# Low parts of the mixers' weight chunks: every fourth one subtracted on GpSimd instead of VectorE

## The chip, the cores and the metric

The kernel runs on one core of a Trainium2 chip. The metric is the device time of one execution in microseconds (us). TensorE is PE in the profile, VectorE is DVE, ScalarE is ACT, GpSimd is POOL, SyncE is SP. Numbers that enter a large product are kept in two parts here: a high part, rounded to the format fp32r, and the low part that the rounding leaves over.

## The reference

256 tokens of width 1024 go through two blocks. The first block has two layers, each a mixer, a layer norm, a feed-forward part (dense in layer 0, eight experts with two chosen per token in layer 1) and another layer norm:

```python
def mixer_block(x, w_in, ...):
    p_swa, p_rwkv, p_fox, p_dsa, p_gate = split_cols(x @ w_in, IN_GROUPS)
    o_swa = swa_branch(*split_cols(p_swa, SWA_SPLITS), sinks)
    o_rwkv = rwkv7_branch(p_rwkv, mu, w0, w_up, a0, a_up, g_up, k_k, k_a, r_k, gn_g, gn_b)
    o_fox = fox_branch(*split_cols(p_fox, FOX_SPLITS), f_bias)
    o_dsa = dsa_branch(*split_cols(p_dsa, DSA_SPLITS))
    gates = jax.nn.sigmoid(p_gate.reshape(B, S, N_BRANCHES, D_MODEL) + gate_bias)
    w_rows = split_cols(w_branch, MIX_WIDTHS, axis=0)
    for i, (o, w) in enumerate(zip((o_swa, o_rwkv, o_fox, o_dsa), w_rows)):
        merged = merged + gates[:, :, i] * (o @ w)
    return merged @ w_out

def first_block(x, ...):
    for layer in range(DEPTH):
        y = mixer_block(x, w_in[layer], ...)
        x = layer_norm(DN_ALPHA * x + y, ln_g[layer, 0], ln_b[layer, 0])
        ...
```

`swa` is attention in a window with sinks, `rwkv7` a recurrence of matrix states with a group norm and a gate at its end, `fox` attention with forget gates, `dsa` attention to the 64 best of the keys that an index score picks. The second block (a mixer of MoBA and gMLP, gated linear attention, cross-attention, SwiGLU) is not touched by the change.

## The kernel before, in words

**Products.** The tokens are two tiles of 128 (`t` = 0, 1). Every activation that enters a weight product is kept as a high part and a low part (`xh`, `xl`), and so is every weight (`H`, `L`). `lin` (L550 on) and `lin_fm` (L576 on) issue three matmuls per step: `xh`·`H`, `xl`·`H`, `xh`·`L`. The third one needs the low part of the weight.

**Weight chunks.** `load` (L512 to L531) brings one chunk, at most 128 x 1024 numbers: SyncE starts its DMA into a half of a `raw` tile (four such halves in the mixers), ScalarE copies it in fp32r into `wh` (through `act`, L445), and VectorE subtracts, `raw` − `wh`, into `wl` (through `sub` and `tt`, L458). There are six pairs of `wh` and `wl`; a pair is free again after the last matmul that reads it (`done`).

**The mixers.** A mixer sets `woven` (`weave`, L425). Its 68 chunks are then loaded ahead, at most four (`LOOK = 4`), as pairs come free (`fill`, `take`). TensorE's instructions and SyncE's weight DMAs keep the order of the program (`keep_in_program_order`); the other engines' order is set by a scheduler, which is why an edit of one helper can move instructions elsewhere. Between the projections the generators of the recurrence (`rwkv_tile`, L1052), `dsa` (L993), `fox` (L954) and `swa` (L941) are pumped on, each step's small products and row operations lying among the large products. Mixer 0 takes the first 305 us of the span, mixer 1 about the stretch from 510 to 830 us.

**Helpers that the steps below name.** `tt` (L458) is a two-input operation of VectorE, `stt` (L455) one with a scalar too, `ts` (L450, L452) one with one input; all run on VectorE unless an engine is passed. `groupnorm` (L1297) ends the recurrence of a tile: sums (L1299, L1307), an inverse root by small operations, then products on 128x256; the product with the gate follows, and TensorE transposes it (L382). `dsa` picks by eight rounds of `max` and `match_replace` (L1019, L1020). `ln_apply` (L1347) normalises tile 0, transposes it and splits it, and then tile 1. GpSimd makes masks at the start (L642, L730), clears buffers for the recurrence (L1180, L1213) and starts some DMAs (L1062, L1063, L1344).

**Holding.** `held` (L533) keeps the subtractions of the next mixer out of a layer norm: after tile 0 is split, `ln_apply` sets `hold = (last, 2)`, so the next two subtractions are free and the following ones may issue only after `last`. `self.last` names the last subtraction, and `rwkv` (L1041) lets three small operations of its constants issue after it.

Of the kernel before, what the change touches and what calls it, by code (L numbers as in the profile page):

```python
# [11 lines left out]
F32 = mybir.dt.float32  # L12
# [77 lines left out]
def specs():  # L90
    sp = {}
    for l in range(2):
        sp[f"win{l}"] = std_chunks(D, win_blocks())
        sp[f"wbr{l}"] = [_kch(_r(k, k + n), b) for k, n in ((0, 4), (4, 2), (6, 2), (8, 2)) for b in _blocks(D)]
        sp[f"wout{l}"] = kfirst_chunks(D, _blocks(D))
        sp[f"xq{l}"] = std_chunks(D, _blocks(D))
        sp[f"xkv{l}"] = std_chunks(D, _blocks(2 * D))
        sp[f"xo{l}"] = kfirst_chunks(D, _blocks(D))
        gu = []
        for b in _short_second(FF):  # L100
            for o in (0, FF):
                gu.append(_kch(_r(0, 8), [c + o for c in b]))
        sp[f"gu{l}"] = gu
        sp[f"dn{l}"] = down_chunks(FF)
    sp["w1"] = std_chunks(D, _short_second(FF))
    sp["w3"] = std_chunks(D, _short_second(FF))
    sp["w2"] = down_chunks(FF)
    sp["evin"] = std_chunks(D, _blocks(2560))
    sp["evo"] = kfirst_chunks(D, _blocks(D))
    sp["odin"] = std_chunks(D, _blocks(3072))  # L110
    sp["odo"] = kfirst_chunks(D, _blocks(D))
    sp["rw"] = [[(_r(0, 8), _r(0, 8))]]
    sp["odg1"] = [[(_r(0, 8), _r(0, 16))]]
    for e in range(8):
        sp[f"e1_{e}"] = std_chunks(D, _short_first(1408))
        sp[f"e3_{e}"] = std_chunks(D, _short_first(1408))
        sp[f"e2_{e}"] = down_chunks(1408)
    return sp
# [82 lines left out]
class Arena:  # L201
# [4 lines left out]
    def __init__(self, tiles, small=0, fit=0):  # L206
        self.t = tiles
        self.small, self.fit = small, fit
        self.at = [np.zeros(t.shape[-1] // self.U, np.int64) for t in tiles]
        self.clock = 0  # L210
        self.used, self.peak = 0, 0
# [51 lines left out]
class Net:  # L263
    def __init__(self, ctx, tc, a, out):
        self.tc, self.nc, self.a, self.out = tc, tc.nc, a, out
        self.sp = specs()
        self.off = {}
        self.cst = ctx.enter_context(tc.tile_pool(name="cst", bufs=1))
        pool = ctx.enter_context(tc.tile_pool(name="ar", bufs=1))
        block = lambda n, dt, w=CH: pool.tile([128, w], dt, name=n, tag=n)  # L270
        self.arena = Arena([block(f"af{i}", F32) for i in range(AF_BLOCKS)], small=SMALL)
        self.arenar = Arena([block("ars", F32R, AR_SMALL)] + [block(f"ar{i}", F32R) for i in range(AR_BLOCKS)], small=8, fit=64)
        self.raws = deque()
        for i in range(RAW):
            r = block(f"raw{i}", F32)
            self.raws.extend(r[:, j:j + RW] for j in range(0, CH, RW))
        self.pairs = deque()
        for i in range(0, PAIRS, 2):
            h, l = block(f"wh{i}", F32R), block(f"wl{i}", F32R)
            self.pairs.extend((h[:, j:j + RW], l[:, j:j + RW]) for j in range(0, CH, RW))  # L280
        self.extra = []
        self.pp = ctx.enter_context(tc.tile_pool(name="pp", bufs=4, space=PSUM))
        self.first = None
        self.hold, self.remap = (None, 0), {}
        self.ahead = AHEAD
        self.woven, self.vt, self.chains, self.loaded, self.todo = False, 0.0, [], deque(), deque()
        self.keys, self.scopes, self.cur = {}, [], None

# [208 lines left out]
    def block(self, name, b, lazy=False):  # L497

        if name not in self.off:
            o, l = 0, []  # L500
            for blk in self.sp[name]:
                l.append([])
                for k, c in blk:
                    l[-1].append(o)
                    o += 128 * len(k) * len(c)
            self.off[name] = l
        if self.woven and not lazy:
            return [partial(self.take, name, c) for c in self.off[name][b]]
        ws = [partial(self.load, name, *c) for c in zip(self.sp[name][b], self.off[name][b])]
        return ws if lazy else [w() for w in ws]  # L510

    def load(self, name, chunk, off):  # L512
        ks, cols = chunk
        ap = self.a[name]
        m = len(ks) * len(cols)
        src = bass.AP(tensor=ap.tensor, offset=ap.offset + off, ap=[[m, 128], [1, m]])
        w = Weight(self.pairs.popleft(), ks, len(cols))
        w.id = name, off
        raw = self.raws.popleft()
        dma = self.nc.sync.dma_start(out=raw[:, :m], in_=src)  # L520
        if self.woven:
            self.tc.keep_in_program_order(dma)
        h, lo = w.pair[0][:, :m], w.pair[1][:, :m]
        with self.tc.high_priority(self.ahead):
            with self.tc.issue_after(self.first.ins) if self.first else nullcontext():
                self.act(h, raw[:, :m])
            with self.held():
                self.last = self.sub(lo, raw[:, :m], h.bitcast(F32))
        self.raws.append(raw)
        return w  # L530

# [1568 lines left out]
```

## Time and profile before

| | |
|---|---|
| median of 3 runs | 2142.77 us |
| the runs | 2140.14 to 2144.49 us |
| the profiled execution | 2144.34 us |
| its span, first to last instruction | 2142.6 us |
| instructions | 31352 |
| mean granted clock of TensorE, of full speed | 0.982 |

The times that the sections below work with are those of the profiled execution, counted from the start of its span. A timeline row gives the start, the time busy, the engine, the line, the operation, what it writes and reads (buffer numbers left out), and in brackets the engine's idle time just before and what ended it. Rows of equal instructions that follow each other are one row with their count. Chunks are counted from 0 in each mixer, in the order of their loading.

### The profile page before, as it was taken

The page shows a single profiled execution, that of the slowest core. Times are in us where ns is not written, and L with a number is a line of the kernel's source. Part 1 is how long each engine was busy: PE and PEld are TensorE (multiplying, and loading weights), DVE is VectorE, ACT ScalarE, POOL GpSimd, SP SyncE. Part 2 cuts the span into 40 slices and gives each one's busy share as a digit, 9 for nine tenths or more (in the row PEclk, how much of TensorE's full clock was granted, in tenths as well). Part 3 has the DMA queues.
Part 4 walks back from the last instruction along what each step waited for, and adds up shares of the span by engine and source line. Part 5 has one row for each costly group of instructions (what it writes and reads, how often), then busy time and mean ns, then how long its engine had stood idle before and what let it go on. Part 6 is the DMA issues. An engine that isn't in the chain of part 4 may idle for free. (4 is left out here: it accounts for less than half of the span.)

```text
span 2142.6 us, 31352 instructions
## 1 busy us (share of the span) xinstructions
PE 2074.1 (97%) x11520; PEld 1699.4 (79%) x11520; DVE 1514.8 (71%) x2952; ACT 1138.3 (53%) x1684; POOL 43.1 (2%) x115
## 2 busy tenths in 40 slices
PE   8989999998998999999999998999999999999999
PEld 7867777886986777888888887877888777778887
DVE  6776677556667579988888898977645657676454
ACT  5433444443444345677777785575544454555442
POOL 1000000000000000000000000000000000000000
PEclk9999999999999999999999999999999999999999
DMA  6532474552544345699999997536555353654561
GB/s 227 173 94 86 156 251 148 187 188 78 171 136 124 106 141 195 222 345 333 344 339 327 333 316 237 170 127 210 178 188 187 105 171 117 205 181 164 177 197 59
DMA packets 118450, 411.91 MB, mean 192 GB/s; under 512 B 13648, under 2 KB 13808, under 8 KB 118288
## 3 DMA queue, kind: packets, MB, share of 16 engines
q1 hardware_dynamic: 113184, 392.91, 54.9%
q0 software_dynamic: 5104, 16.92, 2.5%
q8 instruction: 92, 1.51, 0.3%
q14 instruction: 70, 0.57, 0.1%
HBM read 408.72 MB, written 1.05 MB: 191 GB/s over the span
## 5 line engine op out<-in xcount | busy, mean ns | idle before, releaser
L379 PE MATMUL mm<-wh,ar 128*128 128x512 f32 (+3 forms) x3200 | 982.0, 388 | 11.1 <-PEq L1670 5.1
L379 PEld LDWEIGHTS mm<-wh,ar 128*128 128x128 f32 x3200 | 588.0, 190 | 126.9 <-issue 14.5
L458 DVE TENSOR_TENSOR wl<-raw,wh 128x1024 fp32r<-128x1024 f32 (+3 forms) x464 | 547.5, 1192 | 182.9 <-ACT wh L445 173.3
L445 ACT ACTIVATE wh<-raw 128x1024 fp32r<-128x1024 f32 (+3 forms) x464 | 476.1, 1035 | 279.0 <-PE mm L379 157.3
L379 PE MATMUL mm<-wl,ar 128*128 128x512 f32 (+3 forms) x1600 | 614.7, 384 | 0.0
L458 DVE TENSOR_TENSOR wl<-af,wh 128x1024 fp32r<-128x1024 f32 (+2 forms) x300 | 347.2, 1173 | 151.7 <-ACT wh L445 141.5
L445 ACT ACTIVATE wh<-af 128x1024 fp32r<-128x1024 f32 (+2 forms) x300 | 303.7, 1020 | 153.6 <-PE mm L379 56.3
L379 PE MATMUL ps<-wh,ar 128*128 128x512 f32 x1104 | 349.8, 394 | 2.3 <-ACT ar L445 2.3
L379 PEld LDWEIGHTS mm<-wl,ar 128*128 128x128 f32 x1600 | 304.1, 190 | 55.5 <-issue 0.8
L379 PEld LDWEIGHTS ps<-wh,ar 128*128 128x128 f32 x1104 | 206.3, 188 | 44.8 <-ACT ar L445 3.9
L379 PE MATMUL ps<-wl,ar 128*128 128x512 f32 x552 | 215.4, 390 | 0.0
L379 PE MATMUL mm<-ar,wh 128*128 128x256 f32 x704 | 139.2, 298 | 4.5 <-ACT ar L445 2.7
L382 PE MATMUL pr<-ident,af 128*128 128x128 f32 x584 | 97.8, 290 | 39.6 <-DVE af L458 24.7
L445 ACT ACTIVATE ar<-pr 128x512 fp32r<-128x512 f32 (+1 forms) x118 | 65.9, 567 | 115.3 <-PE pr L382 100.1
L382 PEld LDWEIGHTS pr<-ident,af 128*128 128x128 f32 x584 | 69.7, 146 | 71.4 <-issue 40.1
L379 PEld LDWEIGHTS mm<-ar,wh 128*128 128x128 f32 x704 | 115.0, 200 | 8.8 <-ACT ar L445 3.4
L379 PEld LDWEIGHTS ps<-wl,ar 128*128 128x128 f32 x552 | 103.8, 188 | 20.8
L379 PE MATMUL pr<-wh,ar 128*128 128x512 f32 x352 | 111.6, 395 | 1.2 <-ACT ar L445 1.0
L445 ACT ACTIVATE af<-af 128x512 f32<-128x512 f32 (+6 forms) x132 | 63.5, 491 | 83.1 <-DVE af L458 61.7
L379 PE MATMUL mm<-ar,wl 128*128 128x256 f32 x352 | 102.4, 291 | 0.0
L458 DVE TENSOR_TENSOR af<-af,af 128x512 f32<-128x512 f32 (+2 forms) x166 | 96.5, 595 | 4.4 <-ACT af L445 1.6
L458 DVE TENSOR_TENSOR ar<-pr,ar 128x512 fp32r<-128x512 f32 (+1 forms) x110 | 70.6, 653 | 33.1 <-ACT ar L445 32.6
(198 smaller groups left out, 1685.0 us busy)
## 6 DMA issues: line engine op xcount, KB each, us to landing
af<-in_e_dram SPq DMA_DIRECT2D x127, 512.0 KB, 5.1
raw<-in_win_dram SPq DMA_DIRECT2D x108, 512.0 KB, 4.5
raw<-in_e_dram SPq DMA_DIRECT2D x81, 512.0 KB, 5.0
af<-in_gu_dram SPq DMA_DIRECT2D x56, 512.0 KB, 4.0
af<-in_w_dram SPq DMA_DIRECT2D x42, 512.0 KB, 4.5
raw<-in_xkv_dram SPq DMA_DIRECT2D x32, 512.0 KB, 4.5
raw<-in_gu_dram SPq DMA_DIRECT2D x32, 512.0 KB, 4.6
af<-in_e_dram SPq DMA_DIRECT2D x38, 384.0 KB, 4.9
```

Source lines behind the costliest of these rows:

```text
L379: return self.pe(self.nc.tensor.matmul(out, lhsT=lhsT, rhs=rhs, start=start, stop=stop, skip_group_check=True), lhsT, rhs)
L382: return self.pe(self.nc.tensor.transpose(out, in_, ident), in_, ident, 1)
L445: return self.nc.scalar.activation(out, in_, f, **kw)
L458: return (eng or self.nc.vector).tensor_tensor(out, a, b, op=op)
```

## The change

A counter, `turn`, goes up at every load of the kernel, of the mixers or not. When it reaches 0 of 4 and the load is woven, the subtraction goes to GpSimd. It is not put under `held`, so it doesn't count there, and `self.last` doesn't name it. All other loads are as before.

```diff
@@ -283,6 +283,7 @@
         self.first = None
         self.hold, self.remap = (None, 0), {}
         self.ahead = AHEAD
+        self.turn = 0
         self.woven, self.vt, self.chains, self.loaded, self.todo = False, 0.0, [], deque(), deque()
         self.keys, self.scopes, self.cur = {}, [], None
 
@@ -524,8 +525,12 @@
         with self.tc.high_priority(self.ahead):
             with self.tc.issue_after(self.first.ins) if self.first else nullcontext():
                 self.act(h, raw[:, :m])
-            with self.held():
-                self.last = self.sub(lo, raw[:, :m], h.bitcast(F32))
+            self.turn = (self.turn + 1) % 4
+            if self.woven and self.turn == 0:
+                self.sub(lo, raw[:, :m], h.bitcast(F32), self.nc.gpsimd)
+            else:
+                with self.held():
+                    self.last = self.sub(lo, raw[:, :m], h.bitcast(F32))
         self.raws.append(raw)
         return w
 
```

34 subtractions move, 17 in each mixer: chunks 3, 7, 11, ... 67 in mixer 0, chunks 1, 5, 9, ... 65 in mixer 1. The order of TensorE's and SyncE's instructions stays. Line numbers of the helpers shift by one to five in the changed kernel. Three places show how the order changes.

GpSimd's queue at the start of mixer 0, before. `af` are tiles of the recurrence, the rows clear its buffers and fetch its weights:

```order
L1213 MEMSET af_71 128x64x2
L1213 MEMSET af_71 128x32x4
L1062 DMA af_65<-in_wa_up_dram 128x256
L1344 DMA af_65<-in_rrow_dram 128x512
L1063 DMA af_69<-in_g_up_dram 128x256
L1213 MEMSET af_71 128x16x8
```

And with the change:

```order
L1218 MEMSET af_71 128x64x2
L1218 MEMSET af_71 128x32x4
L459 TENSOR_TENSOR wl_83<-raw_79,wh_82 128x1024
L459 TENSOR_TENSOR wl_81<-raw_79,wh_80 128x1024
L459 TENSOR_TENSOR wl_85<-raw_79,wh_84 128x912
L459 TENSOR_TENSOR wl_83<-raw_79,wh_82 128x1024
L1067 DMA af_65<-in_wa_up_dram 128x256
L459 TENSOR_TENSOR wl_81<-raw_79,wh_80 128x1024
L459 TENSOR_TENSOR wl_85<-raw_79,wh_84 128x1024
L1349 DMA af_65<-in_rrow_dram 128x512
L1068 DMA af_69<-in_g_up_dram 128x256
L459 TENSOR_TENSOR wl_83<-raw_79,wh_82 128x1024
```

Seven subtractions now stand among the clears and DMAs: four ahead of the DMA of `wa_up`, two ahead of those of `rrow` and `g_up`, one behind them.

VectorE in the group norm of tile 0, mixer 0, before (the inverse root of the group norm on 128x4, and the largest row values of an attention on 128x2; the product on 128x8x127 belongs to tile 1 of the recurrence):

```order
L458 TENSOR_TENSOR af_61<-af_61 128x4
L450 TENSOR_SCALAR af_61<-af_61 128x2 x2
L458 TENSOR_TENSOR af_61<-af_61 128x4
L458 TENSOR_TENSOR wl_83<-raw_79,wh_82 128x1024
L455 SCALAR_TENSOR_TENSOR af_61<-af_61 128x4
L758 RECIPROCAL af_61<-af_61 128x2
L458 TENSOR_TENSOR af_67<-af_64 128x8x127
```

And with the change:

```order
L459 TENSOR_TENSOR af_61<-af_61 128x4
L451 TENSOR_SCALAR af_61<-af_61 128x2 x2
L459 TENSOR_TENSOR af_61<-af_61 128x4
L459 TENSOR_TENSOR af_67<-af_64 128x8x127
L456 SCALAR_TENSOR_TENSOR af_61<-af_61 128x4
L763 RECIPROCAL af_61<-af_61 128x2
```

The subtraction of chunk 39 (`wl_83`) has left this stretch.

VectorE in the layer norm ahead of mixer 1, before. `af_62` is a token tile, `af_61` the small numbers of its inverse root, `ar_74` the low part of the split activation:

```order
L458 TENSOR_TENSOR ar_74<-pr,ar_77 128x4x128
L455 SCALAR_TENSOR_TENSOR af_61<-af_61 128x1
L458 TENSOR_TENSOR wl_81<-raw_79,wh_80 128x1024
L452 TENSOR_SCALAR af_62<-af_62,af_61 128x512 x2
L458 TENSOR_TENSOR af_62<-af_62,af_69 128x512 x2
L458 TENSOR_TENSOR af_62<-af_62,af_72 128x512 x2
L458 TENSOR_TENSOR wl_83<-raw_79,wh_82 128x1024
L458 TENSOR_TENSOR wl_81<-raw_78,wh_80 128x1024
L458 TENSOR_TENSOR ar_74<-pr,ar_77 128x4x128 x2
L458 TENSOR_TENSOR wl_83<-raw_78,wh_82 128x1024
```

And with the change, where the subtraction of chunk 2 (`wl_81<-raw_79`) stands earlier still, inside tile 0's inverse root:

```order
L459 TENSOR_TENSOR ar_74<-pr,ar_77 128x4x128
L456 SCALAR_TENSOR_TENSOR af_61<-af_61 128x1
L459 TENSOR_TENSOR wl_83<-raw_79,wh_82 128x1024
L456 SCALAR_TENSOR_TENSOR af_61<-af_61 128x1
L459 TENSOR_TENSOR wl_81<-raw_78,wh_80 128x1024
L453 TENSOR_SCALAR af_62<-af_62,af_61 128x512 x2
L459 TENSOR_TENSOR af_62<-af_62,af_69 128x512 x2
L459 TENSOR_TENSOR af_62<-af_62,af_72 128x512 x2
```

The subtractions of chunks 3 and 4 stand ahead of tile 1's normalisation instead of behind it, and that of chunk 5 (`wl_83<-raw_78`) is in GpSimd's queue.

## Rows read from the trace of the kernel before

**Rows 1.** The page, busy time, share and instructions of each engine over the span
```profile
PE 2074.1 (97%) x11520; PEld 1699.4 (79%) x11520; DVE 1514.8 (71%) x2952; ACT 1138.3 (53%) x1684; POOL 43.1 (2%) x115
```
**Rows 2.** Busy time by stage: us, PE, PEld, DVE, ACT, POOL, PEclk, DMA share, GB/s
```profile
0.00:305.00 305.00, 286.83 (x2106) 231.08 (x2107) 215.08 (x548) 136.16 (x257) 19.80 (x64) 0.97 0.50 163
528.00:830.00 302.00, 286.08 (x2102) 230.70 (x2100) 212.77 (x527) 129.79 (x250) 8.88 (x22) 0.94 0.45 142
148.80:153.60 4.80, 4.80 (x13) 3.82 (x14) 1.87 (x8) 0.86 (x3) 0.00 (x0) 0.50 0.00 0
```
**Rows 3.** Waits of PE, mixer 0 (two rows), mixer 1: total, times, longest us
```profile
PE pr L382 <- DVE af L458: 6.9, 2, 6.5
PE pr L382 <- POOL lev L730: 4.7, 1, 4.7
...
PE pr L382 <- DVE af L458: 12.3, 3, 6.4
```
**Rows 4.** Groups of DVE instructions in mixer 0: busy us, mean ns, idle before
```profile
L458 DVE TENSOR_TENSOR wl<-raw,wh 128x1024 fp32r<-128x1024 f32 x71 | 85.7, 1220 | 27.7 <-ACT wh L445 27.5
```
**Rows 5.** Timeline of PE, both mixers and the norm between
```profile
76.49 0.44 PE L382 MATMUL pr<-ident,af 128*128 128x128 f32 x2 [0.44 <-DVE af L458]
...
148.74 0.66 PE L382 MATMUL pr<-ident,af 128*128 128x128 f32 x2 [6.46 <-DVE af L458]
...
537.45 0.58 PE L379 MATMUL mm<-ar,wh 128*128 128x256 f32 x1 [1.03 <-DVE ar L458]
...
570.35 0.72 PE L379 MATMUL pr<-af,af 64*128 64x128 f32 x8
...
601.36 0.44 PE L382 MATMUL pr<-ident,af 128*128 128x128 f32 x2 [0.45 <-DVE af L458]
...
645.34 0.45 PE L379 MATMUL pr<-af,af 64*64 64x64 f32 x8 [0.96 <-DVE af L450]
...
673.58 0.66 PE L382 MATMUL pr<-ident,af 128*128 128x128 f32 x2 [6.44 <-DVE af L458]
```
**Rows 6.** Timeline of DVE, mixer 0, group norm of tile 0
```profile
141.49 1.22 DVE L458 TENSOR_TENSOR wl<-raw,wh 128x1024 fp32r<-128x1024 f32 x1
...
148.17 0.42 DVE L458 TENSOR_TENSOR af<-af 128x256 f32<-128x256 f32 x1
```
**Rows 7.** Timeline of DVE, mixer 1
```profile
642.74 2.34 DVE L458 TENSOR_TENSOR wl<-raw,wh 128x1024 fp32r<-128x1024 f32 x2
645.00 0.28 DVE L450 TENSOR_SCALAR af<-pr 128x128 f32<-128x128 f32 x1
...
660.71 1.22 DVE L458 TENSOR_TENSOR wl<-raw,wh 128x1024 fp32r<-128x1024 f32 x1
661.85 0.42 DVE L458 TENSOR_TENSOR af<-af 128x256 f32<-128x256 f32 x1
```
**Rows 8.** Timeline of DVE, layer norm ahead of mixer 1
```profile
534.45 2.35 DVE L458 TENSOR_TENSOR wl<-raw,wh 128x1024 fp32r<-128x1024 f32 x2
536.72 1.28 DVE L458 TENSOR_TENSOR ar<-pr,ar 128x512 fp32r<-128x512 f32 x2
```
**Rows 9.** Timeline around chunk 7 of mixer 0: ACT, DVE, PE
```profile
24.35 2.86 ACT L445 ACTIVATE wh<-raw 128x1024 fp32r<-128x1024 f32 x3 [2.82 <-PE mm L379]
...
25.44 4.40 DVE L458 TENSOR_TENSOR wl<-raw,wh 128x1024 fp32r<-128x1024 f32 x4 [5.78 <-ACT wh L445]
...
28.83 0.28 PE L379 MATMUL mm<-ar,wl 128*128 128x256 f32 x1
```
**Rows 10.** Timeline of POOL and DVE, setup at the start
```profile
2.36 0.29 POOL L642 TENSOR_SCALAR_AFFINE_SELECT le<-ones 128x128 f32<-128x128 f32 x1
...
2.86 0.41 POOL L642 TENSOR_SCALAR_AFFINE_SELECT E<-ones 4x256 f32<-4x256 f32 x1
...
4.03 0.28 DVE L458 TENSOR_TENSOR gt<-blk,le 128x128 f32<-128x128 f32 x1
```
**Rows 11.** Timeline of POOL, mixer 0
```profile
88.20 0.54 POOL L1063 DMA_DIRECT2D af<-in_g_up_dram  x1 [10.17 <-DVE af L452]
```

## The prediction

> **What bounds the kernel now.** I read the busy shares first. TensorE is busy for 97% of the span, VectorE for 71%, GpSimd for 2% [rows 1]. So a VectorE that is freer gives time back only where TensorE stands still for it, and GpSimd has room for work. The second view is the table by stage, because the change acts in the two mixers alone. In mixer 0 TensorE is busy for 286.83 of 305.00 us and VectorE for 215.08, in mixer 1 for 286.08 of 302.00 and 212.77 [rows 2]: some 34 us of TensorE idle in both together are all that could ever be won. The third view, the waits of TensorE, says whom it stands still for. By VectorE's `af` tiles it is held 6.9 us in mixer 0, of which one wait is 6.5, and 12.3 us in mixer 1, of which one is 6.4 [rows 3]. Never is it held for long by a low part (`wl`): those are made ahead.
>
> The change takes subtractions from VectorE that last 1.22 us each; the group of mixer 0 shows 71 of them, which fill 85.7 us [rows 4]. 34 of them leave, 41 us of VectorE work. What that is worth stands in the timeline of TensorE, where a matmul bears the idle time before it and what ended it [rows 5]: 6.46 us at 148.74, 6.44 at 673.58, 1.03 at 537.45, 0.96 at 645.34, and 0.44 and 0.45 at 76.49 and 601.36. Before each of these VectorE works through its queue. Only a subtraction standing in that queue, ahead of the instruction that TensorE waits for, counts.
>
> **What goes.** The wait at 148.74 ends with the product at 148.17, the last step of rwkv tile 0's group norm and gate in mixer 0; the queue ahead of it has no gap, and chunk 39's subtraction stands in it at 141.49 [rows 6]. It is one of the 34: **−1.2**. At 645.34 TensorE waits for the copy at 645.00, right behind two subtractions that take 2.34; the second (chunk 33) leaves, and as only 0.96 is waited there: **−1.0** [rows 5, 7]. At 673.58 the same queue as in mixer 0 holds chunk 37's subtraction, at 660.71; it leaves: **−1.2** if nothing takes its place [rows 7].
>
> **What moves.** In the layer norm ahead of mixer 1 the subtractions are told to stay behind tile 0's last instruction. Their counting starts with the ones VectorE still makes, so the order changes: chunks 3 and 4, before behind tile 1's norm (2.35 us at 534.45), now stand ahead of it, and chunk 2 goes forward into tile 0's chain. Two more subtractions ahead of the norm's end are +2.4; the wait of 1.03 at 537.45, which came from these two standing ahead of the split at 536.72, goes: **+1.4** [rows 5, 8].
>
> **What is added: a GpSimd subtraction.** No row has a GpSimd instruction with two inputs. Its selects took 0.29 us for 128 columns and 0.41 for 256, so 0.12 per 128 columns, and 0.41 + 6 × 0.12 = 1.13 us for 1024 columns of one input [rows 10]. From below the price is VectorE's own 1.22, from above three such passes, two reads and a write, 3.4. I take two passes, 2.3, since the reads are what is doubled. [...]
>
> Does the low part still come in time? TensorE takes 286.83 us for 68 chunks, 4.2 each, and chunks are loaded four ahead, so most leads are many us. The tightest that I found is chunk 7: the three casts from 24.35 last 2.86, so the second ends near 26.3, GpSimd would end at 28.5, and TensorE first reads that low part at 28.83 [rows 9]. Nothing is lost at 2.3, 0.9 at 3.4. In VectorE's queue that subtraction was one of four in a row that take 4.40 [rows 9].
>
> GpSimd's own queue: 17 subtractions of each mixer now stand between its memsets and DMAs. One DMA there waits 10.17 us for VectorE and starts at 88.20 [rows 11]; a subtraction behind such a DMA comes some us after its cast, still inside a lead of about four chunks, 17 us. A memset or a DMA behind a subtraction comes 2.3 later at most, and TensorE's only long wait on GpSimd in mixer 0, 4.7 us, is on a select of the setup, ahead of them all [rows 3]. SyncE's queue and TensorE's keep their order. A raw buffer is given back up to 1.1 us later; the DMA share is 0.50 and 0.45 there [rows 2], so I cost that at nothing; without that room it would show as casts that wait for DMA.
>
> **The cost I can't price: whether the two engines hinder each other.** All 34 read two SBUF inputs while VectorE runs its own two-input instructions. Beside GpSimd's selects a 128x128 two-input VectorE instruction took 0.28 us [rows 10], no more than the one-input one of the same size at 645.00 [rows 7]: this speaks for no hindrance, but those selects are short and have one input. So I keep both ends. **Free**: −1.2 − 1.0 − 1.2 + 1.4 = −2.0. **Blocked**: VectorE stands still for a whole GpSimd subtraction wherever it wants a two-input instruction. Then the chain behind 673.58 gets 2.3 − 1.2 = +1.0 instead of −1.2, as the square at 661.85 meets chunk 37 [rows 7]; the norm before mixer 1 meets chunk 5's, up to +2.3; four chains for which TensorE already waits or is just served (76.49, 601.36, and the matmul at 570.35 with its counterpart in mixer 0 [rows 5]) get up to 2.3 − 1.2 = +1.0 each; the gap at 148.74 keeps −1.2, as chunk 39's falls beside reductions and small one-input work, and 645.34 keeps −1.0. Sum: −1.2 − 1.0 + 1.0 + 1.4 + 2.3 + 4.0 = +6.5.
>
> [...]
>
> **Sum.** The row I have and its weakness leave me in the middle: (−2.0 + 6.5) / 2 = +2.2. On the median of the runs, 2142.77, that is **2145.0 us**; the profiled execution took 2144.34, 1.6 above that median, so its own successor would be about 2146.6. A measurement of this kernel can tell about 0.2%, 4.3 us, from no change, so the forecast is no change that can be measured.
>
> **Rivals.** *VectorE blocked in full*: slower. Place: the norm before mixer 1 and the chains named above; price 2.3 per collision; time 2142.8 + 6.5 = 2149.3. It decides if two-input VectorE instructions stretch by over about 1.5 us beside a GpSimd subtraction. For it: every one of the 34 runs beside a VectorE that is busy 70% of the mixer [rows 2]. Against it: the 0.28 row.
>
> [...]
>
> *Late low parts*: GpSimd needs 3.4, chunks like 7 come 0.9 late (twice, 1.8), and half-blocked chains grow by half of 6 × 1.1: 2142.8 + 2.2 + 1.8 + 3.3 = 2150.1. TensorE would then wait on `wl` made by GpSimd.
>
> *Less is done than said*: the new branch holds only while loads are woven, so the FFN, the experts and the second block keep all their subtractions on VectorE. The program's order shows exactly 34 that move, so this is a reason for the smallness of the forecast and not a case of its own.
>
> **Chances.** The forecast, within 0.2% (2138.5 to 2147.1): 0.52. Blocked in full 0.29 and late low parts 0.05: slower 0.34. No hindrance with more given back than I count: faster 0.14. The range goes from 2137, which leaves out the far half of the fast case, to 2153, which takes in the blocked one and the late one and leaves out both at their worst (2142.8 + 6.5 + 6.8 + 1.8 = 2157.9).
>
> **What would show it.** GpSimd: 34 subtractions of 1024 or 912 columns; their mean is my 2.3 or isn't. VectorE: a `wl` of 1024 columns at 1.22, the two-input 128x512 split, two in 1.28 [rows 8]: unchanged means free, means of well over these mean blocked. TensorE: idle of about 5.3 in place of 6.46, none in place of 0.96 at 645.34, more than 1.03 ahead of mixer 1's first projection. The forecast is wrong if two-input instructions on VectorE stretch (slower), if TensorE waits for a `wl` by GpSimd (slower), or if the stretches at 0.50 go (faster).

## The result, and the profile after

The changed kernel takes 2159.14 us (median of 4 runs, 2156.53 to 2160.31) against 2143.32 for the kernel before in the same comparison: ratio 1.0076, 95% interval 1.0064 to 1.0088. It is 15.8 us slower. I had forecast no change, 2145.0, with a range up to 2153.0. Its profiled execution has a span of 2157.0 us, 14.4 more than before.

The work by engine, and the group of GpSimd's new instructions (busy us, mean ns, idle before):

```profile
PE 2076.6 (96%) x11520; PEld 1700.8 (79%) x11520; DVE 1512.5 (70%) x2918; ACT 1138.6 (53%) x1684; POOL 131.0 (6%) x149
...
L459 POOL TENSOR_TENSOR wl<-raw,wh 128x1024 fp32r<-128x1024 f32 x32 | 83.2, 2601 | 275.0 <-ACT wh L446 260.7 <-DVE wl L459 9.4 <-DVE af L459 4.8
```

TensorE runs the 11520 matmuls that it had [rows 1] and is busy 2.5 us longer; the other 11.9 of the 14.4 us are idle. VectorE gave away 34 subtractions of 1.22, 41 us, and its busy time fell by 2.3 us only. Where did the rest go? GpSimd's tile view says that one of its subtractions takes 2157 to 3672 ns, 2399 in the middle, near my 2.3. Beside them, VectorE's instructions read like this (timeline of VectorE and GpSimd, pairs that overlap):

```profile
47.77 2.86 POOL L459 TENSOR_TENSOR wl<-raw,wh 128x1024 fp32r<-128x1024 f32 x1 [7.17 <-ACT wh L446]
48.31 2.61 DVE L453 TENSOR_SCALAR af<-af 128x128 f32<-128x128 f32 x2
...
72.81 2.40 POOL L459 TENSOR_TENSOR wl<-raw,wh 128x1024 fp32r<-128x1024 f32 x1 [9.33 <-ACT wh L446]
73.02 2.34 DVE L456 SCALAR_TENSOR_TENSOR af<-af,af,ad 128x128 f32<-128x128 f32 x1
...
142.85 2.41 POOL L459 TENSOR_TENSOR wl<-raw,wh 128x1024 fp32r<-128x1024 f32 x1 [14.33 <-ACT wh L446]
143.64 1.65 DVE L451 TENSOR_SCALAR af<-af 128x4 int32<-128x4 int32 x1
...
581.05 3.67 POOL L459 TENSOR_TENSOR wl<-raw,wh 128x1024 fp32r<-128x1024 f32 x1 [7.50 <-ACT wh L446]
582.57 2.43 DVE L459 TENSOR_TENSOR af<-af,af 128x256 f32<-128x256 f32 x1
```

Read the ends: 72.81 + 2.40 = 75.21 on GpSimd, and 73.02 + 2.34 = 75.36 on VectorE. In these four pairs VectorE's work ends 0.03 to 0.29 us behind GpSimd's; a tensor_scalar on 128x4 that else takes 0.17 has 1.65. It also goes the other way: at 581.05 GpSimd, at 3.67, lasts 1.3 longer than its 2.4, with a subtraction of VectorE, from 580.65, under way first. Over the whole trace 25 VectorE instructions overlap a GpSimd subtraction and last over 0.15 us longer than the same form does elsewhere, 35.4 us together. So most of the 41 us of relief came back as stalls.

TensorE's order is the same instruction by instruction, so its delay can be read by matching rows (timeline of TensorE; the first row is of the kernel before, the rest are of the changed kernel):

```profile
581.65 0.27 PE L382 MATMUL pr<-ident,af 128*4 128x128 f32 x1
```
```profile
80.84 0.33 PE L383 MATMUL pr<-ident,af 128*128 128x128 f32 x1 [2.63 <-DVE af L459]
...
153.12 0.45 PE L383 MATMUL pr<-ident,af 128*128 128x128 f32 x1 [6.81 <-DVE af L459]
...
542.96 0.58 PE L380 MATMUL mm<-ar,wh 128*128 128x256 f32 x1
...
590.91 0.27 PE L383 MATMUL pr<-ident,af 128*4 128x128 f32 x1 [3.50 <-DVE af L456]
...
613.20 0.33 PE L383 MATMUL pr<-ident,af 128*128 128x128 f32 x1 [1.51 <-DVE af L459]
...
656.14 0.33 PE L380 MATMUL pr<-af,af 64*64 64x64 f32 x4
...
685.96 0.45 PE L383 MATMUL pr<-ident,af 128*128 128x128 f32 x1 [7.18 <-DVE af L459]
```

Against [rows 5] the delay is 80.84 − 76.49 = 4.4 us, still 4.4 at 153.12, 5.5 at 542.96, 9.3 at 590.91 (581.65 before, with no wait), 11.8 at 613.20, 10.8 at 656.14, 12.4 at 685.96. The largest single step is at 590.91, where TensorE had not waited at all and now waits 3.50.

### The profile page after: what moved, and what is told of

It is laid out like the page before. It is cut to its first block, busy times and chain, and to the rows that moved or that the text cites. A ratio compares the mean times of both kernels' runs of the same rounds, so it can differ in the third digit from the quotient of the medians.

```text
span 2157.0 us, 31331 instructions
## 1 busy us (share of the span) xinstructions
PE 2076.6 (96%) x11520; PEld 1700.8 (79%) x11520; DVE 1512.5 (70%) x2918; ACT 1138.6 (53%) x1684; POOL 131.0 (6%) x149
## 5 line engine op out<-in xcount | busy, mean ns | idle before, releaser
L459 DVE TENSOR_TENSOR wl<-raw,wh 128x1024 fp32r<-128x1024 f32 (+2 forms) x430 | 519.4, 1218 | 190.9 <-ACT wh L446 177.1
L459 POOL TENSOR_TENSOR wl<-raw,wh 128x1024 fp32r<-128x1024 f32 (+1 forms) x34 | 87.6, 2578 | 312.9 <-ACT wh L446 298.6
L459 DVE TENSOR_TENSOR af<-af,af 128x512 f32<-128x512 f32 (+2 forms) x166 | 102.0, 628 | 3.7 <-ACT af L446 1.6
```

What stands on the lines that cost most here:

```text
L459: return (eng or self.nc.vector).tensor_tensor(out, a, b, op=op)
```

## The experiments

**Order alone.** The bookkeeping of the change, with the subtraction left on VectorE:

```diff
-            with self.held():
-                self.last = self.sub(lo, raw[:, :m], h.bitcast(F32))
+            self.turn = (self.turn + 1) % 4
+            if self.woven and self.turn == 0:
+                self.sub(lo, raw[:, :m], h.bitcast(F32))
+            else:
+                with self.held():
+                    self.last = self.sub(lo, raw[:, :m], h.bitcast(F32))
```

> All low parts stay on VectorE; only the bookkeeping of the change is kept: the 34 subtractions of the mixers are not held behind the layer norm and are not named as the last one. Port theory (a GpSimd subtraction shuts VectorE out while it reads SBUF): the order in the layer norm costs at most the 1.4 us that I put down for it, so within 0 to 2 us of the kernel before. Rival (the 16 us come from the new order of VectorE's instructions): 10 to 16 us slower than before.

Measured: 2144.98 against 2142.98, ratio 1.0013 (1.0 to 1.0025). "Port theory" is here and below the name for what its bracket says; what lies behind a stall inside the chip, no run shows. The new order of the layer norm is worth 2.0 us by the medians and 5.4 at most by the interval, against 15.8. In its trace TensorE is 0.4 us late ahead of the norm and 2.3 behind it (539.70 against 537.45 [rows 5]). The rest is GpSimd's.

**The hindrance alone.** VectorE does all it did; GpSimd repeats each of the 34 into a buffer of 832 columns (the space that was left):

```diff
+            self.turn = (self.turn + 1) % 4
+            if self.woven and self.turn == 0:
+                self.sub(self.scr, raw[:, :832], h.bitcast(F32)[:, :832], self.nc.gpsimd)
```

> VectorE makes all low parts as before; GpSimd makes each of the 34 subtractions once more, of 832 columns, into a buffer that nobody reads. No engine but GpSimd gets another instruction or another order. Port theory: GpSimd's subtractions last about 2.0 us and VectorE's SBUF-only instructions stand still beside them; as VectorE is relieved of nothing, 8 to 18 us slower than before. Rival (order, or late low parts): within 2 us of before, as no order moves and nobody waits for these results.

Measured: 2171.27, ratio 1.0138 (1.012 to 1.0156), 28.3 us slower. More than I expected, and more than the change itself. Counted as above, 30 VectorE instructions stretch by 43 us (25 by 35 in the changed kernel), and no relief stands against them. VectorE's 68 subtractions of 1024 columns in the first 310 us show it (groups of VectorE in that stretch; 1220 ns before [rows 4]):

```profile
L461 DVE TENSOR_TENSOR wl<-raw,wh 128x1024 fp32r<-128x1024 f32 x68 | 93.3, 1387 | 24.2 <-ACT wh L448 23.9
```

**Writing instead of reading.** GpSimd reads one column, so as to start at the same time, and clears the buffer twice:

```diff
+                self.sub(self.scr[:, :1], raw[:, :1], h.bitcast(F32)[:, :1], self.nc.gpsimd)
+                for _ in range(2):
+                    self.nc.gpsimd.memset(self.scr, 0.0)
```

> As the second kernel of this group, but GpSimd reads only one column of raw and wh (128x1) at each of the 34 places and then clears the buffer of 832 columns twice, so it is as long at work and only writes. Port theory, reads: 0 to 3 us slower than before, no VectorE instruction stretched beside the clears. Rival (any GpSimd work beside VectorE hinders it, or its queue does): 8 to 18 us slower, as with the reads.

Measured: 2143.76, ratio 1.0008 (0.9999 to 1.0018). GpSimd is at work for about as long (groups of GpSimd), and VectorE's subtractions keep their 1220 ns (group of VectorE, first 310 us):

```profile
L536 POOL MEMSET scr<- 128x832 f32 x68 | 54.1, 795 | 4.0 <-POOL scr L461 0.2
L461 POOL TENSOR_TENSOR scr<-raw,wh 128x1 f32<-128x1 f32 x34 | 25.8, 760 | 314.4 <-ACT wh L448 222.5 <-issue 91.9
...
L461 DVE TENSOR_TENSOR wl<-raw,wh 128x1024 fp32r<-128x1024 f32 x71 | 85.7, 1220 | 26.1 <-ACT wh L448 25.9
```

My expectation was not quite right in one thing: some instructions do stretch beside the clears. There are 16, by 7.0 us in all, most of them tensor_scalar or copy, and none a subtraction of a low part, of which 28 overlap a clear.

**Which VectorE instructions are shut out.** Behind the last product, thirteen times: VectorE clears one column of `A`, which releases a GpSimd subtraction, and runs ten equal instructions (`K` keeps them in the order of the program).

```diff
+            for f in kinds:
+                K(v.memset(A[:, 0:1], 1.0))
+                self.sub(self.scr, A[:, :832], Bq[:, :832], nc.gpsimd)
+                for _ in range(n):
+                    K(f())
```

> The kernel before with a test behind its last product: 13 times a GpSimd subtraction of 832 columns is released by VectorE, which then runs ten equal instructions of one kind beside it; results go nowhere. Port theory as after's trace suggests it: stretched by up to 2 us are the two-input instructions from SBUF (tensor_tensor and scalar_tensor_tensor 128x256) and the one-input ones from SBUF to SBUF (tensor_scalar, copy, the small 128x4 ones too); not stretched are those with an input in PSUM, the reduction, max, and the clear. Rival, my prediction's reading (two-input ones alone): tensor_scalar and copy run at their usual 0.2 to 0.4 us. The whole lasts some 40 us more than before.

Measured (timeline of VectorE and, first row, GpSimd; of a kind that is shut out the instruction that met GpSimd's 1.94 us and a later one):

```profile
2140.93 1.94 POOL L460 TENSOR_TENSOR scr<-af,af 128x832 f32<-128x832 f32 x1 [260.17 <-ACT af L447]
2141.49 1.66 DVE L460 TENSOR_TENSOR af<-af 128x256 f32<-128x256 f32 x1 [1.47 <-ACT af L447]
2143.18 0.42 DVE L460 TENSOR_TENSOR af<-af 128x256 f32<-128x256 f32 x1
...
2147.40 2.08 DVE L2092 TENSOR_SCALAR af<-af,af 128x256 f32<-128x256 f32 x1
2149.51 0.35 DVE L2092 TENSOR_SCALAR af<-af,af 128x256 f32<-128x256 f32 x1
...
2158.42 2.04 DVE L457 SCALAR_TENSOR_TENSOR af<-af,af 128x256 f32<-128x256 f32 x1
2160.49 0.48 DVE L457 SCALAR_TENSOR_TENSOR af<-af,af 128x256 f32<-128x256 f32 x1
...
2183.54 1.94 DVE L2099 TENSOR_SCALAR af<-af 128x4 f32<-128x4 f32 x1
...
2199.78 1.97 DVE L2103 TENSOR_TENSOR_SCAN af<-af 128x128 f32<-128x128 f32 x1
```

Shut out until GpSimd ends: the product, scalar_tensor_tensor and scan with two inputs in SBUF, and, with one, tensor_scalar (the three forms fp32, bf16 output with 1.94 instead of 0.29, and 128x4) and copy (1.91 instead of 0.29). Not at all: the kinds of the next view (groups of VectorE in the test; their means are those of the undisturbed instruction).

```profile
L2096 DVE TENSOR_SCALAR af<-pr,af 128x256 f32<-128x256 f32 x10 | 4.8, 484 | 0.3
...
L2098 DVE MAX8 af<-af 128x8 f32<-128x256 f32 x10 | 4.3, 428 | 0.3
L460 DVE TENSOR_TENSOR af<-pr,af 128x256 f32<-128x256 f32 x10 | 4.2, 424 | 0.4
L2097 DVE TENSOR_REDUCE af<-af 128x1 f32<-128x256 f32 x10 | 4.2, 420 | 0.3
...
L2101 DVE MEMSET af<- 128x256 f32 x10 | 2.7, 272 | 1.1
```

So in this test the product and the tensor_scalar with an input in PSUM are free (424 and 484 ns), and so are the reduction, max and the clear (420, 428 and 272 ns), though the first two read SBUF. Two kinds that the test leaves out pass in the changed kernel's trace: a match_replace on 128x256 takes its usual 0.41 at 655.96, beside a subtraction of GpSimd from 655.54 to 658.04, and a reciprocal on 128x2 takes 0.17 at 105.75, beside one from 105.10 to 107.49. The rival, my reading in the prediction, falls.

**Nine, and the other 25.** The set is a table by mixer and chunk:

```diff
+            self.cn += 1
+            if self.woven and self.cn in ((7, 11, 15, 23, 39), (5, 13, 17, 21))[self.mx]:
+                self.sub(lo, raw[:, :m], h.bitcast(F32), self.nc.gpsimd)
+            else:
```

> Only nine of the 34 subtractions go to GpSimd: chunks 7, 11, 15, 23, 39 of mixer 0 and 5, 13, 17, 21 of mixer 1, those whose collision stands in the changed kernel's trace right ahead of a later start of TensorE. Theory (what counts is whom a GpSimd subtraction shuts out, not how many there are): the steps of delay at these places in the changed kernel add up to some 12 us, so 8 to 14 us slower than before. Rival (each of the 34 costs about the same): 9/34 of 16, so 3 to 6 us slower.

> The other 25 of the 34 subtractions go to GpSimd, the nine of the kernel before this one stay on VectorE. Theory: 0 to 5 us slower than before, though GpSimd is at work for 60 us. Rival (each costs about the same): 25/34 of 16, so 10 to 13 us slower.

Measured: nine of them 2162.95, ratio 1.0102 (1.0081 to 1.0122), 18.7 us slower; the other 25, 2143.15, ratio 0.9998 (0.9986 to 1.0009). The two differences add to 17.6, about the change's 15.8, so the cost of the change is that of nine instructions. It overshoots my 14 us. The 25 are no loss, though VectorE is held up for 20.5 us beside them too: none of that shows as lost time.

**Shorter pieces.** Each GpSimd subtraction of the changed kernel in four of 256 columns:

```diff
+                for j in range(0, m, 256):
+                    k = min(j + 256, m)
+                    self.sub(lo[:, j:k], raw[:, j:k], h.bitcast(F32)[:, j:k], self.nc.gpsimd)
```

> The changed kernel with each GpSimd subtraction cut into four of 256 columns; all other engines keep the instructions and the order of the changed kernel. Theory (VectorE is shut out for one GpSimd instruction, and gets its turn between two): a collision costs at most some 0.7 us instead of 2.4, so 3 to 10 us slower than before, clearly faster than the change. Rival (GpSimd's total time on the port counts, or VectorE waits for the whole row of them): 14 to 25 us slower than before.

Measured: 2155.10, ratio 1.0063 (1.0043 to 1.0082), 10.9 us slower by the medians, just beyond the 10 of the theory. The interval, 9 to 18 us, reaches into the rival's 14 to 25 and into the change's own 14 to 19, so it is not shown that the pieces help. VectorE does not reliably get its turn between two pieces. Its lost time falls from 35.4 to 30.1 us only, in 61 instructions instead of 25, and in places it waits for all four (timeline of GpSimd and VectorE):

```profile
815.12 2.81 POOL L459 TENSOR_TENSOR wl<-raw,wh 128x256 fp32r<-128x256 f32 x4
...
815.17 3.85 DVE L459 TENSOR_TENSOR wl<-raw,wh 128x1024 fp32r<-128x1024 f32 x1 [1.14 <-ACT wh L446]
```

**Other ways to shorten TensorE's two waits of 6.5 us.** First, with all low parts on VectorE, a later transpose (`yield 8.0` behind the group norm becomes `yield 10.0`).

> The kernel before, with all low parts on VectorE; only the recurrence waits for 10 instead of 8 us of TensorE work between its group norm and the transpose of its result, so TensorE has more chunks to multiply while VectorE works off its queue. Theory (TensorE's two waits of 6.5 us are waits for VectorE's chain, which the change wanted to shorten): 2 to 8 us faster than before. Rival (the wait moves to the next user of the chain): within 2 us of before.

Measured: 2155.36, ratio 1.0056 (1.0034 to 1.0078): slower by 11.1 us, a miss. The two waits did shrink, to 4.08 each (at 149.50 and 675.53), but two that the kernel before doesn't have came, 4.28 at 284.64 and 7.10 at 812.74. So the row of TensorE's waits on VectorE's `af` tiles has ten with 30.3 us in all, instead of eight with 24.7 in the whole kernel before. TensorE's order is another one here, and the other half of the 11.1 us I did not follow.

```profile
PE pr L382 <- DVE af L458: 30.3, 10, 7.1
```

Second, the subtractions of chunks 37 to 39 are issued behind the group norm instead of in the middle of it, and third, 24 of the harmless 25 go to GpSimd as well (the first two lines stand in `take`: what is left over by then is issued where the program takes one of these chunks):

```diff
+        if w.cn in (37, 38, 39):
+            self.flush()
...
+            if self.woven and self.cn in (37, 38, 39):
+                self.late.append(low)
...
         self.mul(of, of, gm)
+        self.flush()
         yield 8.0
```

> All low parts on VectorE, as before; but the subtractions of chunks 37, 38 and 39 of each mixer are issued only behind the product that ends tile 0's group norm and gate, so they leave the queue ahead of TensorE's two waits of 6.5 us without going to GpSimd. This measures the term -1.2 of my prediction by itself. Theory (a subtraction in that queue costs its 1.2 us): two of them leave the queue in each mixer, 2 to 6 us faster than before. Rival (the chain ahead of these waits is not VectorE's queue): within 1 us of before.

> The kernel before this one, and the 25 subtractions of the earlier run on GpSimd too, without chunk 37 of mixer 1, whose collision stood ahead of the wait at 673.58. Theory (only collisions ahead of a wait of TensorE cost, and a shorter queue ahead of a wait gains): 4 to 9 us faster than before. Rival (VectorE's free time outside the waits is worth nothing): like the run before, 0 to 6 us faster, no better than it.

Measured: the second 2142.80, ratio 0.9993 (0.9982 to 1.0004), the third 2142.28, ratio 0.9985 (0.9975 to 0.9995). The second shows nothing that can be told from no change, and its trace says why (timeline of TensorE, both waits, and of VectorE ahead of the first):

```profile
148.84 0.66 PE L383 MATMUL pr<-ident,af 128*128 128x128 f32 x2 [6.12 <-ACT af L455]
...
671.79 0.66 PE L383 MATMUL pr<-ident,af 128*128 128x128 f32 x2 [6.11 <-ACT af L455]
```
```profile
142.28 1.22 DVE L468 TENSOR_TENSOR wl<-raw,wh 128x1024 fp32r<-128x1024 f32 x1
...
148.28 0.41 DVE L468 TENSOR_TENSOR af<-af 128x256 f32<-128x256 f32 x1
...
148.88 1.21 DVE L468 TENSOR_TENSOR wl<-raw,wh 128x1024 fp32r<-128x1024 f32 x1
```

The waits fell by 0.3 each, from 6.46 and 6.44 [rows 5]. Only one subtraction left the queue in each mixer, chunk 39's (at 148.88 behind the product); chunk 38's still stands at 142.28, chunk 37's at 137.13. In the place that came free VectorE runs two scalar_tensor_tensor of 0.34 more, so from chunk 36's subtraction to the product it needs 13.17 us (135.11 to 148.28) instead of 13.78 (134.39 to 148.17), and the same in mixer 1. The rows put the end of the waits down to ScalarE, but its instruction ends at 148.70 and VectorE's product at 148.70 too, and TensorE starts 0.15 behind the product as it did before: that ScalarE's chain ends next is not shown. The third gains 2.2 us by its medians, 1 to 5 by its interval, and I had expected 4 to 9. It is the only version whose interval lies on the fast side of the kernel before, by 0.15%, and its 2142.28 can't be told from the second's 2142.80.

## Why the prediction was wrong

**Right.** Work on VectorE counts only where TensorE stands still for it (the 25 show that, at a ratio of 0.9998); GpSimd's price (2.4 measured, 2.3 taken); the wait at 645.34, which went (656.14 has none, and the delay falls from 11.8 to 10.8); the layer norm's order at +1.4, for which the run with the order alone shows 2.0 with an interval from 0 to 5 us, and its trace 1.9 over the norm; that GpSimd's queue and its DMAs didn't matter (the clears at the same 34 places cost 0.8, not clear of noise). Chunk 7 alone came a little late: its subtraction lasted to 29.27 where TensorE wants it at about 28.8, and less than 1 us was lost.

**The step that failed is the cost that I couldn't price.** I took the middle between free and blocked, +2.2, on a row of 0.28 us beside GpSimd's selects. The blocked end had it right: two-input instructions stand still until GpSimd is done (2.43 at 582.57 for a product that takes 0.42 undisturbed). But that end, +6.5, was itself less than half of the 15.8, for two reasons. (Its five terms of 2.3 − 1.2 are 1.1 each and not 1.0, so it should read +7.0; and the 71 subtractions of [rows 4] are 64 of mixer 0 and seven of the part behind it. Neither moves the forecast by more than 0.3.)

*Who is blocked.* I let one-input instructions pass, so chunk 39's collision "beside small one-input work" cost nothing and left −1.2. The tensor_scalar of 1.65 at 143.64 ate that gain: the wait is 6.81 instead of 6.46. At 48.31 and ahead of the wait at 685.96 it is also a tensor_scalar that stands still (2.61 for two of them, and 2.50 at 671.62). The test by kinds shows the same for tensor_scalar and copy: 2.08 instead of 0.35 for a tensor_scalar on 128x256 and 1.91 instead of 0.29 for a copy, against an undisturbed 484 ns for the tensor_scalar with its input in PSUM.

*Where.* I looked for collisions ahead of waits that the kernel before already had. A stall of 2.4 us makes new ones. The costliest, 3.7 us, is at 590.91, where [rows 5] has no row since TensorE didn't wait there at all; behind the 3.50 us without work TensorE's granted clock is 0.66 of full speed in the mean from 591 to 596, where it was 1.00 before (busy time by stage, us, PE, PEld, DVE, ACT, POOL, PEclk, DMA share, GB/s; changed kernel first, then before):

```profile
591.00:596.00 5.00, 5.00 (x28) 4.66 (x28) 1.91 (x6) 0.27 (x1) 0.00 (x0) 0.66 0.59 197
```
```profile
582.00:588.00 6.00, 6.00 (x50) 5.75 (x49) 5.10 (x12) 1.89 (x4) 0.00 (x0) 1.00 0.61 177
```

How much of the miss is "where"? Matched row by row, the steps of TensorE's delay at the places that the blocked sum names are 2.2 at 80.84, 0.7 at 575.95 and 0.4 at its counterpart in mixer 0, 1.1 at 613.20, 2.1 over the norm, 0.7 at 685.96, 0.3 at 153.12 and −1.0 at 656.14. Together that is 6.5, what the sum had, and that is in part luck: the norm was priced at 3.7, and 153.12 at −1.2. The rest lies where it names none: 3.7 at 590.91 and 1.5 right behind it, in the stretch at 0.66; 1.0 each at 50.82 and 725.08; 0.7 at 674.17; 2.0 behind the mixers; less some 2 that come back in between.

**The gain was too large as well.** −1.2 for a subtraction in the queue ahead of the two long waits was arithmetic on VectorE's queue. Where one left it without a collision, the queue shortened by 0.6 only, as the scheduler put other instructions in its place, and the waits shrank by 0.3.

**Of the rivals**, the first was right in kind, with its point (stretch of over 1.5 us, measured up to 2.2), and short in size: 2149.3 against 2159.1. I gave it 0.29: one weak row of the trace spoke against it (0.28 us beside two selects of 64x32 that took 0.34 and 0.35, where a stall of 2.4 could not show), and I weighed the row too high. The late low parts fall: TensorE's wait for a low part by GpSimd is 0.2 us in all. The stretch at 0.50 [rows 2] did not go: the granted clock is 0.52 from 153.2 to 158.0 in the changed kernel, behind a wait of 6.81 us instead of 6.46. That a shorter wait brings the clock back, on which the fast case in my range rested, no run shows.

**Open.** Behind the mixers the delay grows by another 2 us, from 12.3 at 841.06 (828.77 before) to 14.3 at the end, with no GpSimd subtraction there, as the last starts at 819.2; runs of one kernel differ by as much, and no run here tells the two apart. The nine alone came out slower than all 34 (18.7 against 15.8 in two comparisons, with intervals of 17 to 26 and 14 to 19 us, which overlap); that the others bring a small gain would explain it, and the third version fits, but no run was made for it.

## What to carry to other kernels

Before work goes from VectorE to GpSimd, list what VectorE runs during it by operand: in this kernel GpSimd's reading stopped tensor_tensor, scalar_tensor_tensor, scan, tensor_scalar and copy that worked on SBUF alone until GpSimd's instruction had ended (1.66 to 2.08 us in the test by kinds, against 0.16 to 0.48 undisturbed), and let reductions, max, match_replace, clears and what had an input in PSUM pass at their usual 0.27 to 0.48 us, and so 41 us of relief cost 35 us of stalls. For each moved instruction ask whom it meets and whether the bound engine waits for that one, not only where it waits already but in every chain with less slack than the stall: here nine of 34 placements made all of the loss, and the other 25 were harmless.

## What the runs showed of the hardware that I had not expected

- A small instruction of VectorE stood about as long as a larger one: a tensor_scalar on 128x4, 0.17 us alone, took 1.94, and one on 128x256, 0.35 alone, 2.08, each beside a subtraction of GpSimd that lasts 1.94.
- GpSimd pays too: its subtraction at 581.05, with one of VectorE under way first, took 3.67 us where the median of the changed kernel is 2.40, and one of 832 columns took up to 4.31 where VectorE made the same ones too, against 1.94 in the test by kinds.
- Two clears of 832 columns at the same 34 places cost 0.8 us in all, with an interval that takes in 0, where reading of that size cost 28.3.
- Cutting GpSimd's instruction in four didn't let VectorE in reliably: at 815.17 it waited through four pieces, 3.85 us for a subtraction of 1.22.
